# Ranks of the chosen keys: Sign on ScalarE with a table of biases, in place of comparisons of 2048 elements on VectorE

## The chip, the cores and the metric

The kernel runs on one core of one Trainium2 chip. The metric is the device time of one execution in microseconds (us), and a version is judged by the median of its runs. Engines are named as the profile names them: PE (TensorE), PEld (its weight loads), DVE (VectorE), ACT (ScalarE), POOL (GpSimd), SP (SyncE, which here only issues transfers).

## The reference, cut to what matters

Two layers, each of which adds a mixer of three kinds of attention and then an expert retrieval to `x` (256 tokens of 2048 numbers). The change sits in the retrieval. For each token and each of 8 heads it scores 128 keys twice, keeps the 16 best of each side, forms sums of pairs, keeps the 16 best pairs and turns each into the number of one of 16,384 experts:

```python
top_s, top_i = lax.top_k(s, PEER_TOPK)
cand_s = (top_s[..., 0, :, None] + top_s[..., 1, None, :]).reshape(..., 256)
cand_i = (top_i[..., 0, :, None] * PEER_KEYS + top_i[..., 1, None, :]).reshape(..., 256)
best_s, best_j = lax.top_k(cand_s, PEER_TOPK)
idx = jnp.take_along_axis(cand_i, best_j, axis=-1)
g = jax.nn.softmax(best_s, axis=-1)
...
a = jnp.einsum('td,tkd->tk', xt, u[it])
hsel = jax.nn.gelu(a) * gt
y = jnp.einsum('tk,tkd->td', hsel, vv[it])
```

## The kernel before, in words

**The stream of u.** The kernel does not gather the rows of `u`. In each layer it multiplies all 16,384 experts' rows with all 256 tokens: 128 blocks (`q`) of 128 experts, 1 MB each, loaded by SP into the tile `raw` (three buffers at most), and each block is worked in two half-blocks (`k`), 256 in a layer. A half-block is transposed on DVE (line 1274, `uT`), copied to a rounded high part on ACT (line 251, `hi`), has its low part formed by a subtraction on DVE or POOL (line 256, `lo`), and goes through 24 matmuls (lines 1308 and 1310, tile `acc`). After every second block ACT applies the gelu (line 1319, `at`) and the result is written to a large array `Gd` in device memory. Loads, preparation and matmuls run in the order of one loop, `run`: in each turn it prepares the half-block two ahead, multiplies the present one, and then calls `tick`.

**The routing beside it.** The choice of experts is a generator, `route`, put into the list `side`. `tick` runs it to its next `yield`, so a piece of routing stands between the half-blocks on every engine:

```python
def tick():
    for g in side[:SIDE_W[0]]:
        try:
            next(g)
        except StopIteration:
            side.remove(g)
```

So one `yield` is one half-block of the stream. While `r["routing"]` is set, the low parts of three half-blocks in four are formed on POOL, otherwise on DVE. `route` works the tokens in two halves (`hf`). Near the end of each half stand the lines that are changed: the position `bj` of each of the 16 chosen pairs of a head is taken apart into a rank on each side (`abf[:, 0]` the start of the row of pairs, `abf[:, 1]` the place in it), each rank is compared with 16 candidates (line 1019, 8 heads x 16 choices x 16 candidates = 2048 elements per partition, tile `oh`), the result is multiplied by the key numbers `tif` (line 1023) and summed (line 1033). For side 0 the comparison is "at least the start of the row", and `tif` holds differences of neighbouring keys, so that the sum is the wanted key; for side 1 it is equality. Lines 1036 and 1037 put both keys and the token together to `idx`, the address of one element of `Gd`.

**The scatter.** When both halves are done, three yields later, POOL issues one indirect DMA for each of 8 heads x 16 choices x 2 halves (line 1050, `Gd<-g,idx`), each of which adds 128 weights `g` into `Gd`: 256 in a layer, of which 32 are held back until six rows of `v` have been fetched (line 1360). Near the end of the stream, at block 122, SP loads the weights of the last three blocks back from `Gd` (line 1301, `gs`), and this load must wait for the scatter:

```python
if q == NQ - 6 and k == 0:
    gt = va["g"] = r["up"].tile([P, NS, T], F32, name="gs")
    for h in range(2):
        SP.dma_start(gt[:, :, h * P:(h + 1) * P], gav[0][:, NQ - NS:, h])
```

The loads of the later blocks of `u` stand behind it in SP's queue. Two more generators, `marks` (line 1123, `over`) and `lists` (lines 1207 to 1265), follow `route` and find out which experts were chosen; at block 108 `drain()` runs whatever is left of them at once. Then the stage of `v` begins.

Of the kernel before, what the change touches and what calls it, by code (L numbers as in the profile page):

```python
# [27 lines left out]
AF = mybir.ActivationFunctionType  # L28
OP = mybir.AluOpType
# [4 lines left out]
P = 128  # L34
# [7 lines left out]
E = 16384  # L42
NQ = E // P

C_ID, C_IO, C_TP, C_ST = 0, 128, 144, 146
NPERS = 162
NS = 3
NW = (NQ - NS) // 2 * 2
PRE = ((1, 0), (1, 1), (2, 0), (2, 1), (0, 0), (0, 1))
# [7 lines left out]
def shape_constants():  # L57
    pers = np.zeros((P, NPERS), np.float32)
    pers[:, C_ID:C_ID + P] = np.eye(P)
    pers[:, C_IO:C_IO + 16] = np.arange(16)  # L60
    pers[:, C_TP] = np.arange(P)
    pers[:, C_TP + 1] = np.arange(P) + T
    pers[:, C_ST:C_ST + 16] = [16 * a if a < 4 else 64 + 4 * (a - 4) for a in range(16)]
    mix = np.zeros((P, NMIX), np.float32)
    p = np.arange(P)
    inv = (10000.0 ** (-np.arange(32, dtype=np.float64) / 32)).astype(np.float32)
    ang = inv[p % 32][:, None] * np.arange(T, dtype=np.float32)[None, :]
    mix[:, M_COS:M_COS + T] = np.cos(ang.astype(np.float64))
    mix[:, M_SIN:M_SIN + T] = np.where((p % 64) < 32, -1.0, 1.0)[:, None] * np.sin(ang.astype(np.float64))
    for hf in range(2):  # L70
        dist = np.abs(p[:, None] + hf * P - np.arange(T)[None, :]).astype(np.float32)
        mix[:, M_DIST + hf * T:M_DIST + (hf + 1) * T] = np.where(dist <= 128, dist, 1e32)
    c = p % 64
    st = np.clip(c - 8, 0, 48)
    kc = np.arange(64)[None, :]
    ok = (kc >= st[:, None]) & (kc < st[:, None] + 16)
    mix[:, M_BM:M_BM + 64] = np.where(ok, 0.0, -1e30)
    m = np.arange(P)[None, :]
    k = p[:, None]
    mix[:, M_SW:M_SW + P] = (m // 64 == k // 64) & (m % 64 == (k % 64 + 32) % 64)  # L80
    mix[:, M_DUP:M_DUP + P] = (k < 64) & (m % 64 == k)
    mix[:, M_DSW:M_DSW + P] = (k < 64) & (m % 64 == (k + 32) % 64)
    mix[:, M_REV:M_REV + P] = (m // 64 == k // 64) & (m % 64 == 63 - k % 64)
    lst = np.zeros((P, NLST), np.float32)
    lst[:, L_LE:L_LE + P] = k <= m
    lst[:, L_GT:L_GT + P] = k > m
    lst[:, L_LT:L_LT + P] = k < m
    lst[:, L_IO:L_IO + 512] = np.arange(512)
    lst[:, L_JC:L_JC + P] = -(m * P + k + 0.5)
    lst[:, L_BA:L_BA + 32] = 512.0 * np.arange(32)  # L90
    return pers, mix, lst
# [3 lines left out]
def hybrid_parallel_heads_peer_encoder_kernel(ctx, tc, x, ln1, w_in, a_sink, b_rel_bias, c_q_norm, c_kv_norm,  # L95
# [4 lines left out]
    V, S, G, TE, SP = nc.vector, nc.scalar, nc.gpsimd, nc.tensor, nc.sync  # L100
# [16 lines left out]
    pers = pools.new("pers")  # L117
# [3 lines left out]

    CP = pers.tile([P, NPERS], F32, name="CP")
    SP.dma_start(CP, c_pers)
    ident = CP[:, C_ID:C_ID + P]
    iota16 = CP[:, C_IO:C_IO + 16]
    start16 = CP[:, C_ST:C_ST + 16]
    gains = pers.tile([P, 112], F32, name="gains")
    onecol = pers.tile([P, 1], F32, name="onecol")
    V.memset(onecol, 1.0)
# [740 lines left out]
    def peer(l, m):  # L870
        r = {}
# [46 lines left out]
        def evac_q(a):  # L918
            rp = r["rp"]
            qh = rp.tile([P, 8, T], F32R, name="qh", tag="oh0")  # L920
            ql = rp.tile([P, 8, T], F32R, name="ql", tag="oh1")
            r["routing"] = True
            side.append(route(a, qh, ql))
# [25 lines left out]
        def route(a, qh, ql):  # L949
# [19 lines left out]
            for hf in range(2):  # L969
                top = rp.tile([P, 8, 2, 16], F32, name="top", tag="top", bufs=2)  # L970
                ti = rp.tile([P, 8, 2, 16], U32, name="ti", tag="ti", bufs=2)
                tif = rp.tile([P, 8, 2, 16], F32, name="tif", tag="tif", bufs=2)
# [34 lines left out]
                abf = rp.tile([P, 2, 8, 16], F32, name="abf", tag="abf")  # L1007
# [2 lines left out]
                V.tensor_scalar(ab[:, 0], ab[:, 0], 3, None, op0=OP.bitwise_or)  # L1010
                V.tensor_tensor(ab[:, 1], bj, ab[:, 0], op=OP.bitwise_and)
                V.tensor_copy(abf[:, 1], ab[:, 1])
                V.tensor_tensor(tif[:, :, 0, 1:], ti[:, :, 0, 1:], ti[:, :, 0, :15], op=OP.subtract)
                i12 = rp.tile([P, 2, 8, 16], F32, name="i12", tag="i12")
                yield
                ohs = []
                for c in range(2):
                    oh = rp.tile([P, 8, 16, 16], F32, name="oh", tag=f"oh{c}")
                    V.tensor_tensor(oh, abf[:, c, :, :, None].to_broadcast([P, 8, 16, 16]),
                                    (iota16 if c else start16)[:, None, None, :].to_broadcast([P, 8, 16, 16]),  # L1020
                                    op=OP.is_equal if c else OP.is_ge)
                    yield
                    V.tensor_tensor(oh, oh, tif[:, :, c, None, :].to_broadcast([P, 8, 16, 16]), op=OP.mult)
                    ohs.append(oh)
                    yield
# [8 lines left out]
                    yield  # L1034
                i1, i2 = (i12[:, c].rearrange("p h k -> p (h k)") for c in range(2))
                V.scalar_tensor_tensor(i1, i1, 128.0, i2, op0=OP.mult, op1=OP.add)
                V.tensor_scalar(r["idx"][:, hf], i1, 512.0, CP[:, C_TP + hf:C_TP + hf + 1], op0=OP.mult, op1=OP.add)
                yield
                found.append((top, cand, best))
            r["routing"] = False  # L1040
# [516 lines left out]
```

## Time and profile before

| | us |
|---|---|
| runs of the kernel before (3) | 3339.32, 3327.32, 3314.28 |
| median | 3327.32 |
| the profiled execution: its own time | 3324.39 |
| the profiled execution: span from the first to the last instruction | 3322.6 |

The profile and all rows below are of the one profiled execution. It lies 2.93 us under the median of the runs, and the runs lie 25 us apart. Start times in the rows are us from the span's start; a window A:B means that stretch of the span. A row of a timeline gives the start, the time the instructions took, engine, line, operation, what it writes and reads, and in brackets how long the engine had been idle before it and for what. Idle time of an engine that nothing waits for costs nothing.

### The profile page before, as it was taken

The numbers are of one execution on the slowest core, as the hardware profiler recorded it, in microseconds if no ns is written. First come the engines' busy times: TensorE is split into PE (matmuls) and PEld (weight loads), VectorE is DVE, ScalarE is ACT, GpSimd is POOL, SyncE is SP. The second block draws the span as 40 slices with busy tenths as digits, with TensorE's granted clock in tenths as the row PEclk, the third lists the DMA queues.
The fourth block names the chain that finished last, engine by engine and source line by source line (L and its number), as shares of the span: only waits on it lengthen the run. The fifth ranks groups of instructions, "written<-read, shape, count | busy, mean of one in ns | idle before, by whom it ended". The sixth has DMA issues, their size and how long they took to land. (4 is left out here: it accounts for less than half of the span.)

```text
span 3322.6 us, 58212 instructions
## 1 busy us (share of the span) xinstructions
PE 3085.5 (93%) x21677; PEld 2852.7 (86%) x21677; DVE 2439.9 (73%) x3613; ACT 1701.7 (51%) x2827; POOL 1805.3 (54%) x1135
## 2 busy tenths in 40 slices
PE   8998998999999977999999989999899999889998
PEld 8997898899999976888889977989899998877886
DVE  6676578987879855777776666599977787667776
ACT  5554443356757424555554544433576564345554
POOL 3110045588888873666531010365788888736662
PEclk9999999999999988999999999999999999999999
DMA  5677688899999996888835776988899999968885
GB/s 193 197 219 212 169 182 180 184 180 190 185 186 201 177 210 219 338 312 302 301 124 179 231 182 191 195 184 179 178 182 189 183 199 172 228 198 331 303 310 180
DMA packets 438648, 702.14 MB, mean 211 GB/s; under 512 B 104568, under 2 KB 237384, under 8 KB 414088
## 3 DMA queue, kind: packets, MB, share of 16 engines
q1 hardware_dynamic: 256912, 434.08, 54.3%
q0 software_dynamic: 112304, 228.13, 23.8%
q10 hardware_dynamic: 69064, 35.36, 4.4%
q8 instruction: 190, 3.11, 0.4%
q14 instruction: 178, 1.46, 0.2%
HBM read 627.95 MB, written 69.47 MB: 210 GB/s over the span
## 5 line engine op out<-in xcount | busy, mean ns | idle before, releaser
L1308 PE MATMUL acc<-x2h,hi 128*128 128x256 f32 x4096 | 1012.2, 286 | 31.0 <-ACT hi L251 15.3
L1050 POOL DMA_INDIRECT Gd<-g,idx x512 | 928.8, 1814 | 171.1 <-issue 151.7
L1308 PE MATMUL acc<-x2l,hi 128*128 128x256 f32 x4096 | 997.2, 282 | 0.3 <-issue 0.3
L251 ACT ACTIVATE hi<-uT 128x1024 fp32r<-128x1024 f32 x512 | 543.2, 1061 | 725.9 <-DVE uT L1274 616.0
L1274 DVE STREAM_TRANSPOSE uT<-raw 128x1024 f32<-128x1024 f32 x512 | 634.9, 1240 | 303.1 <-DMA raw<-in_peer_u_dram 217.3
L1308 PEld LDWEIGHTS acc<-x2h,hi 128*128 128x128 f32 x4096 | 783.5, 191 | 37.2 <-ACT hi L251 20.0
L1308 PEld LDWEIGHTS acc<-x2l,hi 128*128 128x128 f32 x4096 | 781.9, 191 | 1.3 <-issue 1.3
L1310 PE MATMUL acc<-x2h,lo 128*128 128x256 f32 x4096 | 583.5, 285 | 99.2 <-DVE lo L256 76.3
L1310 PEld LDWEIGHTS acc<-x2h,lo 128*128 128x128 f32 x4096 | 523.2, 191 | 119.1 <-DVE lo L256 87.1
L166 DVE TENSOR_TENSOR vl<-vr,vh 128x1024 fp32r<-128x1024 f32 x356 | 425.8, 1223 | 140.9 <-ACT vh L165 133.9
L256 POOL TENSOR_TENSOR lo<-uT,hi 128x1024 fp32r<-128x1024 f32 x116 | 302.5, 2609 | 395.2 <-DMA raw<-in_peer_u_dram 194.0
L256 DVE TENSOR_TENSOR lo<-uT,hi 128x1024 fp32r<-128x1024 f32 x396 | 470.0, 1187 | 21.4 <-PE acc L1310 11.3
L165 ACT ACTIVATE vh<-vr 128x1024 fp32r<-128x1024 f32 x356 | 366.5, 1054 | 141.0 <-PE y L156 129.7
L152 PE MATMUL y<-vh,dh 128*128 128x512 f32 x1032 | 406.6, 394 | 18.8 <-ACT vh L165 13.5
L256 DVE TENSOR_TENSOR lo<-raw,hi 128x1024 fp32r<-128x1024 f32 (+1 forms) x240 | 291.5, 1222 | 160.8 <-ACT hi L251 60.2
L156 PE MATMUL y<-vh,dl 128*128 128x512 f32 x1032 | 405.2, 393 | 0.0
L251 ACT ACTIVATE hi<-raw 128x1024 fp32r<-128x1024 f32 (+1 forms) x240 | 245.4, 1034 | 239.7 <-DMA raw<-in_w_o_dram 79.3
L1360 POOL DMA_INDIRECT vr<-in_peer_v_dram,iv x160 | 217.1, 1357 | 172.5 <-ACT vh L165 78.9
L161 PE MATMUL y<-vl,dh 128*128 128x512 f32 x1032 | 294.4, 392 | 0.3
L152 PEld LDWEIGHTS y<-vh,dh 128*128 128x128 f32 x1032 | 196.0, 190 | 63.4 <-ACT vh L165 22.7
L161 PEld LDWEIGHTS y<-vl,dh 128*128 128x128 f32 x1032 | 194.8, 189 | 43.0 <-DVE vl L166 2.5
L156 PEld LDWEIGHTS y<-vh,dl 128*128 128x128 f32 x1032 | 196.1, 190 | 40.9
(400 smaller groups left out, 4268.4 us busy)
## 6 DMA issues: line engine op xcount, KB each, us to landing
raw<-in_peer_u_dram SPq DMA_DIRECT2D x1024, 256.0 KB
raw<-in_w_in_dram SPq DMA_DIRECT2D x64, 512.0 KB
Gd<-z SPq DMA_DIRECT2D x32, 1024.0 KB
raw<-in_w_o_dram SPq DMA_DIRECT2D x32, 1024.0 KB
Gd<-at ACTq DMA_DIRECT2D x124, 256.0 KB
raw<-in_w_in_dram SPq DMA_DIRECT2D x64, 256.0 KB
raw<-in_peer_w_q_dram SPq DMA_DIRECT2D x64, 256.0 KB
raw<-in_w_in_dram SPq DMA_DIRECT2D x32, 416.0 KB
```

What stands on the lines that cost most here:

```text
L152: TE.matmul(o, lh, rh, start=start, stop=False, skip_group_check=shared)
L156: TE.matmul(o, ll, rh, start=False, stop=False, skip_group_check=shared)
L161: TE.matmul(o, lh, rl, start=False, stop=stop, skip_group_check=shared)
L165: S.activation(hi, src, AF.Copy)
L166: V.tensor_tensor(lo, src, R32(hi), op=OP.subtract)
L251: S.activation(view(h), src, AF.Copy)
L256: (eng or V).tensor_tensor(view(lo), src, R32(view(h)), op=OP.subtract)
L1050: d = G.indirect_dma_start(out=Gd[:], out_offset=bass.IndirectOffsetOnAxis(ap=r["idx"][:, hf, i:i + 1], axis=0), in_=r["g"][:, hf, i:i + 1 ...
L1274: V.transpose(t.rearrange("p (c e i) -> p c e i", c=8, e=4), rv.rearrange("p e (c j) -> p c e j", c=8))
L1308: TE.matmul(o, hi[:, c * P:(c + 1) * P], xx, start=k == 0 and c == 0 and n == 0, stop=False)
L1310: TE.matmul(o, lo[:, c * P:(c + 1) * P], xT(k * 8 + c)[0], start=False, stop=k == 1 and c == 7)
L1360: G.indirect_dma_start(out=raw, out_offset=None, in_=peer_v.rearrange("l e d -> (l e) d"), in_offset=at_(r[iv][:, c, m:m + 1]))
```

## The change: what it does

The two comparisons of 2048 elements on DVE go. In their place ACT fills `oh` in 16 slices for each side, one for each candidate `k`: `Sign(abf + bias_k)`, with the bias 0.5 minus the candidate read from a new table in the constants (`C_SB`, 32 columns of the tile `CP`). Each such instruction has 128 elements per partition and writes them 16 elements apart. A sign is +1 or -1, so both sides now use differences of neighbouring keys, with the first entry of `tif` the sum of the first and the last key; the sum is then twice the wanted key, and line 1037's factor 512 becomes 256. A `yield` stands after every eighth Sign, so that a side has three yields where it had two.

```diff
-                V.tensor_tensor(tif[:, :, 0, 1:], ti[:, :, 0, 1:], ti[:, :, 0, :15], op=OP.subtract)
+                V.tensor_tensor(tif[:, :, :, 1:], ti[:, :, :, 1:], ti[:, :, :, :15], op=OP.subtract)
+                V.tensor_tensor(tif[:, :, :, 0], ti[:, :, :, 0], ti[:, :, :, 15], op=OP.add)
                 i12 = rp.tile([P, 2, 8, 16], F32, name="i12", tag="i12")
                 yield
                 ohs = []
                 for c in range(2):
                     oh = rp.tile([P, 8, 16, 16], F32, name="oh", tag=f"oh{c}")
-                    V.tensor_tensor(oh, abf[:, c, :, :, None].to_broadcast([P, 8, 16, 16]),
-                                    (iota16 if c else start16)[:, None, None, :].to_broadcast([P, 8, 16, 16]),
-                                    op=OP.is_equal if c else OP.is_ge)
-                    yield
+                    for k in range(16):
+                        S.activation(oh[:, :, :, k], abf[:, c], AF.Sign,
+                                     bias=CP[:, C_SB + 16 * c + k:C_SB + 16 * c + k + 1])
+                        if k % 8 == 7:
+                            yield
                     V.tensor_tensor(oh, oh, tif[:, :, c, None, :].to_broadcast([P, 8, 16, 16]), op=OP.mult)
                     ohs.append(oh)
                     yield
...
-                V.tensor_scalar(r["idx"][:, hf], i1, 512.0, CP[:, C_TP + hf:C_TP + hf + 1], op0=OP.mult, op1=OP.add)
+                V.tensor_scalar(r["idx"][:, hf], i1, 256.0, CP[:, C_TP + hf:C_TP + hf + 1], op0=OP.mult, op1=OP.add)
```

The table of biases, and its place in the constants:

```diff
-C_ID, C_IO, C_TP, C_ST = 0, 128, 144, 146
-NPERS = 162
+C_ID, C_IO, C_TP, C_ST, C_SB = 0, 128, 144, 146, 162
+NPERS = 194
...
+    pers[:, C_SB:C_SB + 16] = 0.5 - pers[:, C_ST:C_ST + 16]
+    pers[:, C_SB + 16:C_SB + 32] = 0.5 - np.arange(16)
```

How the instructions stand on ACT in the first layer, first half of the tokens, from the Exp of the routing on; before:

```order
L1005 ACT_TABLE_LOAD
L1005 ACTIVATE e<-e 128x128
L251 ACTIVATE hi<-uT 128x1024 x3
L1319 ACT_TABLE_LOAD
L1319 ACTIVATE at<-acc 128x512
L1325 DMA Gd<-at 512x1x128
L251 ACTIVATE hi<-uT 128x1024 x4
```

and now, where line 1321 is what was line 1319:

```order
L1005 ACT_TABLE_LOAD
L1005 ACTIVATE e<-e 128x128
L251 ACTIVATE hi<-uT 128x1024
L1021 ACTIVATE oh<-abf,CP 128x128 x8
L251 ACTIVATE hi<-uT 128x1024
L1021 ACTIVATE oh<-abf,CP 128x128 x8
L251 ACTIVATE hi<-uT 128x1024
L1321 ACT_TABLE_LOAD
L1321 ACTIVATE at<-acc 128x512
L1327 DMA Gd<-at 512x1x128
L251 ACTIVATE hi<-uT 128x1024
L1021 ACTIVATE oh<-abf,CP 128x128 x8
```

Each batch of eight Signs stands between two high parts of the stream; a fourth batch follows one `hi` later. The number of table loads in the whole program is the same in both, and none stands at a Sign.

On DVE at the same place, from the last step of the ranks to the weights' sum `rden`; before:

```order
L1013 TENSOR_TENSOR tif<-ti 128x8x15
L1274 STREAM_TRANSPOSE uT<-raw 128x1024
L1019 TENSOR_TENSOR oh<-abf,CP 128x2048
L1274 STREAM_TRANSPOSE uT<-raw 128x1024
L256 TENSOR_TENSOR lo<-uT,hi 128x1024
L1023 TENSOR_TENSOR oh<-oh,tif 128x2048
L1274 STREAM_TRANSPOSE uT<-raw 128x1024
L1019 TENSOR_TENSOR oh<-abf,CP 128x2048
L1274 STREAM_TRANSPOSE uT<-raw 128x1024
L1023 TENSOR_TENSOR oh<-oh,tif 128x2048
L1274 STREAM_TRANSPOSE uT<-raw 128x1024
L1027 TENSOR_REDUCE rden<-e 128x8
```

and now (1276 is what was 1274, 1025 what was 1023, 1029 what was 1027):

```order
L1013 TENSOR_TENSOR tif<-ti 128x16x15
L1014 TENSOR_TENSOR tif<-ti 128x16
L1276 STREAM_TRANSPOSE uT<-raw 128x1024 x2
L256 TENSOR_TENSOR lo<-uT,hi 128x1024
L1276 STREAM_TRANSPOSE uT<-raw 128x1024
L1025 TENSOR_TENSOR oh<-oh,tif 128x2048
L1276 STREAM_TRANSPOSE uT<-raw 128x1024 x3
L256 TENSOR_TENSOR lo<-uT,hi 128x1024
L1025 TENSOR_TENSOR oh<-oh,tif 128x2048
L1276 STREAM_TRANSPOSE uT<-raw 128x1024
L1029 TENSOR_REDUCE rden<-e 128x8
```

Five transposes of the stream stood between `tif` and `rden`; now there are seven.

On POOL in the first layer, from the clearing of the lists to the first scatter; before:

```order
L256 TENSOR_TENSOR lo<-uT,hi 128x1024 x10
L968 MEMSET ie 128x768
L968 MEMSET iv 128x768
L256 TENSOR_TENSOR lo<-uT,hi 128x1024 x48
L1049 ISA
L1050 DMA Gd<-g,idx 8389120x1
```

and now:

```order
L256 TENSOR_TENSOR lo<-uT,hi 128x1024 x10
L968 MEMSET ie 128x768
L968 MEMSET iv 128x768
L256 TENSOR_TENSOR lo<-uT,hi 128x1024 x51
L1051 ISA
L1052 DMA Gd<-g,idx 8389120x1
```

The first scatter stands four half-blocks of the stream later, and three of their low parts are POOL's.

## Rows read from the trace of the kernel before

**Rows 1.** The page's first part: busy us (share of the span) x instructions
```profile
PE 3085.5 (93%) x21677; PEld 2852.7 (86%) x21677; DVE 2439.9 (73%) x3613; ACT 1701.7 (51%) x2827; POOL 1805.3 (54%) x1135
```
**Rows 2.** Windows: length, busy us (instructions) of PE, PEld, DVE, ACT, POOL, clock, DMA, GB/s
```profile
547.00:576.00 29.00, 21.72 (x170) 20.28 (x170) 28.90 (x23) 10.31 (x11) 17.88 (x6) 1.00 0.85 177
...
685.00:1160.00 475.00, 453.83 (x3943) 445.74 (x3943) 392.74 (x485) 294.62 (x669) 407.59 (x222) 0.99 0.99 187
```
**Rows 3.** SP's queue, waits in window 1200:1260: us in total, times, longest
```profile
SPq L1301 <- DMA Gd<-g,idx: 12.7, 1, 12.7
```
**Rows 4.** The same in window 2880:2930, the second layer
```profile
SPq L1301 <- DMA Gd<-g,idx: 0.2, 1, 0.2
```
**Rows 5.** Timeline of SP's queue at the load of gs, first and second layer
```profile
1249.00 0.93 SPq L1301 DMA_DIRECT2D gs<-Gd  x2
...
2919.08 0.92 SPq L1301 DMA_DIRECT2D gs<-Gd  x2
```
**Rows 6.** Timeline of POOL: first and last scatter of each layer
```profile
684.91 1.73 POOL L1050 DMA_INDIRECT Gd<-g,idx  x1 [0.20 <-issue]
...
1245.53 2.08 POOL L1050 DMA_INDIRECT Gd<-g,idx  x1 [0.30 <-issue]
...
2361.22 1.71 POOL L1050 DMA_INDIRECT Gd<-g,idx  x1 [0.19 <-issue]
...
2913.37 1.56 POOL L1050 DMA_INDIRECT Gd<-g,idx  x1 [0.30 <-issue]
```
**Rows 7.** Groups of POOL in 680:1260: busy, mean ns, idle before and why
```profile
L1050 POOL DMA_INDIRECT Gd<-g,idx x256 | 468.7, 1831 | 86.7 <-issue 75.8 <-DMA vr<-in_peer_v_dram,ivr 9.9 <-DMA Gd<-g,idx 0.3
```
**Rows 8.** Timeline of DVE behind the wait for the scatter, first layer
```profile
1258.22 1.25 DVE L1274 STREAM_TRANSPOSE uT<-raw 128x1024 f32<-128x1024 f32 x1 [12.04 <-DMA raw<-in_peer_u_dram]
```
**Rows 9.** Timeline of DVE at the changed lines, first layer, first half
```profile
547.49 1.23 DVE L1274 STREAM_TRANSPOSE uT<-raw 128x1024 f32<-128x1024 f32 x1
548.65 2.24 DVE L1019 TENSOR_TENSOR oh<-abf,CP 128x2048 f32<-128x2048 f32 x1
...
553.08 2.28 DVE L1023 TENSOR_TENSOR oh<-oh,tif 128x2048 f32<-128x2048 f32 x1
...
556.44 3.30 DVE L1019 TENSOR_TENSOR oh<-abf,CP 128x2048 f32<-128x2048 f32 x1
...
560.83 3.29 DVE L1023 TENSOR_TENSOR oh<-oh,tif 128x2048 f32<-128x2048 f32 x1
564.04 1.23 DVE L1274 STREAM_TRANSPOSE uT<-raw 128x1024 f32<-128x1024 f32 x1
```
**Rows 10.** Timeline of ACT at the same place
```profile
548.82 1.06 ACT L251 ACTIVATE hi<-uT 128x1024 fp32r<-128x1024 f32 x1 [2.37 <-DVE uT L1274]
...
557.71 1.28 ACT L1319 ACT_TABLE_LOAD   x1
559.00 0.60 ACT L1319 ACTIVATE at<-acc 128x512 f32<-128x512 f32 x1
```
**Rows 11.** Timeline of ACT later, a high part and four Relus with a bias
```profile
766.84 1.06 ACT L251 ACTIVATE hi<-uT 128x1024 fp32r<-128x1024 f32 x1 [2.62 <-DVE uT L1274]
767.80 1.27 ACT L1123 ACTIVATE over<-s_sb,nb 128x128 bf16<-128x128 f32 x4
```
**Rows 12.** Groups of ACT, shapes kept apart: busy us, mean ns of one
```profile
L251 ACT ACTIVATE hi<-uT 128x1024 fp32r<-128x1024 f32 x512 | 543.2, 1061 | 725.9 <-DVE uT L1274 616.0 <-issue 43.5 <-PE acc L1310 32.5
...
L1123 ACT ACTIVATE over<-s_sb,nb 128x128 bf16<-128x128 f32 x512 | 162.4, 388 | 19.7 <-ACT at L1319 17.3 <-issue 2.4
...
L1005 ACT ACTIVATE e<-e 128x128 f32<-128x128 f32 x4 | 1.2, 312 | 0.0
```
**Rows 13.** Groups of DVE, shapes apart; the first reads elements 16 bytes apart
```profile
L1092 DVE TENSOR_TENSOR below<-cand,best 128x384 f32<-128x384 f32 x4 | 3.4, 842 | 0.0
...
L1092 DVE TENSOR_TENSOR below<-cand,best 128x512 f32<-128x512 f32 x4 | 2.7, 680 | 0.0
```
**Rows 14.** Transfers issued in window 685:1160: KB each
```profile
raw<-in_peer_u_dram SPq DMA_DIRECT2D x300, 256.0 KB
```

More of the change, by code (lines that the diff above doesn't have):

```diff
@@ L124, in hybrid_parallel_heads_peer_encoder_kernel @@
     ident = CP[:, C_ID:C_ID + P]
-    iota16 = CP[:, C_IO:C_IO + 16]
-    start16 = CP[:, C_ST:C_ST + 16]
     gains = pers.tile([P, 112], F32, name="gains")
```

## The prediction

> **What bounds the kernel now.** The page's first part comes first: PE is busy for 93% of the span [rows 1], which reads like a kernel bound by matmuls. The windows say something else for the stage that the change touches. Around the changed lines DVE is busy for 28.90 of 29.00 us while PE has 21.72; later in the same stage, where the scatter runs, the 16 DMA engines are busy to 0.99 and DVE to 393 of 475 us [rows 2]. So DVE sets the pace for some 30 us in each half of the tokens, and transfers set it behind that.
>
> What ends the stage is a third thing, and the waits of SP's queue show it. In the first layer the load of `gs` waits 12.7 us for the scatter [rows 3] and goes out at 1249.00 [rows 5]; the loads of `u` behind it come late, and DVE then stands idle for 12.04 us [rows 8]. In the second layer the same load waits 0.2 us [rows 4]. The timeline of POOL shows why: the scatter starts at 684.91 and its last instruction at 1245.53, one behind the other [rows 6], 256 of 1.831 us with 86.7 us between them [rows 7]. That is a chain of 563 us (1245.53 + 2.08 - 684.91) which nothing shortens when the rest is faster, and it hangs on the end of the routing. What the change does to the time is therefore read from one number: when the first scatter can start.
>
> How much each layer feels of it: in the first layer the load of `gs` goes out 1.39 us behind the end of the last scatter (1249.00 - 1247.61), and SP was waiting, so a later scatter is a later end, one for one. In the second the last scatter ends at 2914.93; with the same 1.39 us it would have let the load go at 2916.3, and the load went at 2919.08 [rows 5, 6]. So the second layer has 2.8 us to spare.
>
> **The change part by part.** *Removed from DVE:* two comparisons in each half and layer, eight in all, 2.24 us where POOL is quiet and 3.30 us where its subtraction runs beside them [rows 9]. The four turns of the stream with a comparison or a multiplication in them took 564.04 - 547.49 = 16.55 us [rows 9].
>
> *Added to DVE:* the sum for the first entry of `tif`, and 240 elements for 120 in the difference. By the smallest rows of this kind I put both at 0.35 us a half, in front of everything that follows, so it counts.
>
> *Added to ACT:* 32 Signs a half. The nearest row is the Relu of line 1123: the same 128 elements, the same bias from a column. One takes 388 ns [rows 12], four in a row 1.27 us [rows 11], so each further one takes (1.27 - 0.388) / 3 = 0.294 us, and eight behind a `hi` lengthen the queue by 8 x 0.294 = 2.35 us. A `hi` takes its place for 0.96 us (767.80 - 766.84) [rows 11].
>
> *The new chain.* ACT has only 10.31 of 29.00 us of work there [rows 2], which looks like cover. But the Signs come in four batches between five `hi`, and in ACT's order the table load and the gelu stand among them. From the first `hi` at 548.82 [rows 10]: `hi` and eight Signs twice, 2 x (0.96 + 2.35) = 6.6, to 555.4; then the multiplication on DVE, 2.28 [rows 9], and the next transpose, 1.23, to 558.9 (ACT does a `hi`, the table load of 1.28 and the gelu of 0.60 [rows 10] in that time); again twice `hi` and eight Signs, 6.6, to 565.5; the second multiplication, 2.3 to 3.3, to 567.8 or 568.8. It ended at 564.04. With the 0.35 us that is 4.1 to 5.1 us later in each half; I take 4.8. Meanwhile six half-blocks went by and not four, so nothing of the stream is lost: what is lost is that the routing's next pieces stand two half-blocks later.
>
> *Bounds of this term.* Below: if the Signs vanish behind the stream, six turns go by at its pace. In the window of the scatter 300 quarter-megabyte loads, 150 half-blocks, took 475 us [rows 14], 3.17 us each; six are 19.0 us, 2.5 more than 16.55, with the 0.35 us 2.8. Above: the Signs write one element in each 64 bytes, which no row of ACT shows. On DVE, line 1092 takes 680 ns for 512 neighbouring elements, and the comparison of 2048 took 2.24 us, so 1.02 ns an element; 384 would take 550 ns, but where they are read 16 bytes apart they take 842 [rows 9, 13], 0.76 ns an element more. If ACT's writes pay the same, a Sign takes 0.10 us more, 32 take 3.1, and a half is 7.9 us later. I keep 4.8, since the Relu's row has the same engine, operand and size. [...]
>
> *The scatter itself.* Its instructions last longer when DVE runs beside them: their mean is 1.831 us [rows 7] against 1.56 us for the quick ones [rows 6], 69 us in all over the 563 / 3.17 = 178 half-blocks that run beside it. Four fewer are beside it now, which gives back 4 x 0.39 = 1.6 us.
>
> *At nothing:* the 16 KB of constants more at the start, since the transfer is short and the start is not what the stage ends on; the Signs' tables, as the built program has as many table loads as before; and the four half-blocks by which `marks` and `lists` end later. Their last step stood four turns ahead of `drain` and now falls into it, the first piece there; nothing queues up, and POOL still has scatters to do then. If that cover were gone, the six fetches of `v` would wait for the lists.
>
> **The sum.** In each layer the scatter starts 2 x 4.8 = 9.6 us later and runs 1.6 us shorter: 8.0. The first layer pays 8.0, the second 8.0 - 2.8 = 5.2, together 13. Against the profiled execution's own 3324.39 that is 3337.6; that execution lies 2.9 us under the median of the runs, so I predict **3340 us**, 0.4% slower.
>
> **The rivals.** *The stream sets the end, and DVE's relief counts (not slower).* The changed lines are where DVE is full, and DMA stands at 0.85 there against 0.99 later [rows 2]. If transfers could make up that difference over the two stretches of some 29 us in each layer, (0.99 - 0.85) x 29 x 4 = 16 us would come off: 3308 against the profiled execution, 3311 against the median. It decides if the load of `gs` no longer waits, that is if the scatter, started later, still ends before SP gets there. Against it: in the first layer it would have to end 12.7 us earlier, and it hangs on the same routing. I give it 0.12.
>
> *Writes 64 bytes apart are dear.* At the upper bound above, 7.9 us a half: (15.8 - 1.6) + (15.8 - 1.6 - 2.8) = 25.6, 3350, or 3353 against the median. If each element cost four times the 0.84 ns that `hi` shows ((1061 - 312) ns over 896 elements [rows 12]), a Sign would take 0.32 us more, a half 10.3 us: 15.1 us a half, 54 in all, 3382. [...] I give the first 0.22 and the second 0.05. The first is a matter of size, the sign stays.
>
> *The Signs hide.* At 2.8 us a half, the scatter starts 5.6 us later, 4.0 net; the first layer pays 4.0, the second 1.2: 3330, or 3333 against the median. What speaks for it is ACT's idle time [rows 2]; against it that a multiplication waits for 16 Signs in a row. Chance 0.15.
>
> **How the numbers follow.** My own case has 0.46, and these are all. Runs of the kernel before lie within 25 us, so a measurement can hardly tell less than 1% (33 us) from no change. Against the median, the likeliest cases span 3333 to 3353; a median of three such runs may move by some 10 us to either side, which gives **3323 to 3363**. Within that range lie my case, the hiding and most of the first dear case; outside are the gain and the dearest writes, under 2 in 10. Slower by over 1% (above 3360.6) holds the dearest writes, a part of the first dear case and of the noise: 0.11. Faster by over 1% needs twice what the first rival gives: 0.03. Within 1%: 0.86.
>
> **What would show it.** Right: the first multiplication on DVE waits for Signs; the Signs' mean is 0.39 us; `rden` follows the last step of `tif` some 5 us later than it did; the first scatter starts some 10 us later after the stream's first transpose; SP's wait at `gs` is near 22 us in the first layer and 7 in the second. Wrong: no wait at `gs` (the first rival), Signs of 0.5 us or more (the second), or a scatter whose own length changes by more than a few us, since I hold it fixed. The prediction would also fail if the time behind `gs` were not passed on one for one.

## The result, and the profile after

The changed kernel takes 3352.21 us (3343.72 to 3366.13), the kernel before, beside it on the same chip, 3331.37 us (3314.28 to 3348.75). The ratio is 1.0064, with a 95% interval of 1.0043 to 1.0085: slower by 21 us, between 14 and 28. That is inside the range of the prediction and on its side, but more than its 13 us. The profiled execution has a span of 3347.6 us, 25.0 more than before.

The first part of the page, busy us of each engine, answers to [rows 1]. DVE gave up 26.7 us (2439.9 - 2413.2) and ACT took 37.6 more (1739.3 - 1701.7), which is 128 x 0.294:

```profile
PE 3099.3 (93%) x21677; PEld 2869.1 (86%) x21677; DVE 2413.2 (72%) x3603; ACT 1739.3 (52%) x2955; POOL 1808.7 (54%) x1141
```

Windows of the changed kernel, columns as in [rows 2]:

```profile
547.00:576.00 29.00, 23.16 (x182) 21.93 (x183) 22.21 (x21) 21.82 (x46) 16.97 (x7) 1.00 0.87 188
685.00:1160.00 475.00, 447.54 (x3840) 437.83 (x3839) 384.73 (x481) 289.75 (x665) 402.44 (x224) 0.99 0.96 183
```

Around the changed lines DVE is busy for 22.21 of 29.00 us where it was full with 28.90, and the transfers rise from 0.85 to 0.87 (177 to 188 GB/s). So the engine that set the pace there was relieved, and in this window the stream went a little faster. Little of that lasts: by the 89th of its 256 transposes in a layer it is later than before (below).

What ends the stage is read as before. Waits of SP's queue at the load of `gs`, now line 1303, in windows 1200:1300 and 2900:2960 (us in total, times, longest), answering to [rows 3, 4]:

```profile
SPq L1303 <- DMA Gd<-g,idx: 10.2, 1, 10.2
...
SPq L1303 <- DMA Gd<-g,idx: 9.6, 1, 9.6
```

Timeline of SP's queue at that load in both layers [rows 5]:

```profile
1252.88 0.93 SPq L1303 DMA_DIRECT2D gs<-Gd  x2
...
2943.69 0.92 SPq L1303 DMA_DIRECT2D gs<-Gd  x2
```

Timeline of POOL, first and last scatter of each layer [rows 6]:

```profile
700.61 1.73 POOL L1052 DMA_INDIRECT Gd<-g,idx  x1 [0.20 <-issue]
...
1249.58 1.91 POOL L1052 DMA_INDIRECT Gd<-g,idx  x1 [0.30 <-DMA Gd<-g,idx]
...
2385.39 1.71 POOL L1052 DMA_INDIRECT Gd<-g,idx  x1 [0.19 <-issue]
...
2940.65 1.68 POOL L1052 DMA_INDIRECT Gd<-g,idx  x1 [0.30 <-issue]
```

The starts are to be counted from the first transpose of the stream of `u` in their layer. That stands at 419.83 and 2099.20 before and at 423.17 and 2109.52 after. So the scatter starts 277.4 and 275.9 us behind it, where it was 265.1 and 262.0: 12.4 and 13.9 us later. Now both layers wait at `gs`, and the second one did not. The last transpose of `u` follows 17.2 and 17.7 us behind that load (1270.05 and 2961.36); before, in the layer that waited, it was 16.4 (1265.41). So where SP waits, the end of the scatter sets the end of the stage.

Timeline of DVE at the changed lines, first layer, first half [rows 9] and then second half:

```profile
550.25 2.36 DVE L1276 STREAM_TRANSPOSE uT<-raw 128x1024 f32<-128x1024 f32 x2
...
558.44 2.29 DVE L1025 TENSOR_TENSOR oh<-oh,tif 128x2048 f32<-128x2048 f32 x1 [3.27 <-ACT oh L1021]
...
568.78 2.29 DVE L1025 TENSOR_TENSOR oh<-oh,tif 128x2048 f32<-128x2048 f32 x1 [0.93 <-ACT oh L1021]
570.99 1.24 DVE L1276 STREAM_TRANSPOSE uT<-raw 128x1024 f32<-128x1024 f32 x1
...
660.84 1.24 DVE L1276 STREAM_TRANSPOSE uT<-raw 128x1024 f32<-128x1024 f32 x1
...
671.65 2.29 DVE L1025 TENSOR_TENSOR oh<-oh,tif 128x2048 f32<-128x2048 f32 x1 [4.65 <-ACT oh L1021]
...
683.24 2.29 DVE L1025 TENSOR_TENSOR oh<-oh,tif 128x2048 f32<-128x2048 f32 x1 [3.23 <-ACT oh L1021]
685.45 1.24 DVE L1276 STREAM_TRANSPOSE uT<-raw 128x1024 f32<-128x1024 f32 x1
```

Each multiplication waits for Signs, which is a wait that the kernel before did not have. The first half takes 570.99 - 550.25 = 20.7 us where it took 16.55; the second 685.45 - 660.84 = 24.6 where the trace of before has 16.56. Timeline of ACT in that second half shows why it is dearer [rows 10]:

```profile
663.27 1.28 ACT L1321 ACT_TABLE_LOAD   x1
664.56 0.60 ACT L1321 ACTIVATE at<-acc 128x512 f32<-128x512 f32 x1
665.19 0.52 ACTq L1327 DMA_DIRECT2D Gd<-at  x1
665.76 2.56 ACT L1021 ACTIVATE oh<-abf,CP 128x128 f32<-128x128 f32 x8 [0.60 <-ACT at L1321]
668.13 1.04 ACT L251 ACTIVATE hi<-uT 128x1024 fp32r<-128x1024 f32 x1
669.07 2.54 ACT L1021 ACTIVATE oh<-abf,CP 128x128 f32<-128x128 f32 x8
...
679.47 0.57 ACT L1321 ACTIVATE at<-acc 128x512 f32<-128x512 f32 x1
680.07 0.52 ACTq L1327 DMA_DIRECT2D Gd<-at  x1
680.64 2.57 ACT L1021 ACTIVATE oh<-abf,CP 128x128 f32<-128x128 f32 x8 [0.60 <-ACT at L1321]
```

In the first half the table load and the gelu stand between two multiplications, while DVE has stream to do. Here the table load, the gelu and its transfer stand right ahead of the first batch, and a second gelu with its transfer ahead of the last one. In both places DVE is the one that waits.

Groups of ACT, shapes apart (busy us, mean ns), answering to [rows 12]:

```profile
L1125 ACT ACTIVATE over<-s_sb,nb 128x128 bf16<-128x128 f32 x512 | 162.3, 388 | 19.5 <-ACT at L1321 19.5
...
L1021 ACT ACTIVATE oh<-abf,CP 128x128 f32<-128x128 f32 x128 | 40.9, 494 | 2.4 <-ACT at L1321 2.4
```

A Sign lasts 494 ns, 106 more than the Relu. But eight behind one another take 2.54 to 2.57 us, so each further one costs (2.56 - 0.494) / 7 = 0.295 us, the Relu's own step. Signs overlap, and what a single one lasts longer is paid once in eight.

### The profile page after: what moved, and what is told of

Its sections match the earlier page's. It is cut to its first block, busy times and chain, and to the rows that moved or that the text cites. A ratio compares the mean times of both kernels' runs of the same rounds, so it can differ in the third digit from the quotient of the medians.

```text
span 3347.6 us, 58338 instructions
## 1 busy us (share of the span) xinstructions
PE 3099.3 (93%) x21677; PEld 2869.1 (86%) x21677; DVE 2413.2 (72%) x3603; ACT 1739.3 (52%) x2955; POOL 1808.7 (54%) x1141
```

## The experiments

Three parts of the change can be told apart: each half has two turns more (a comparison had one `yield`, 16 Signs have two), ACT's queue has 32 Signs more, and DVE waits for them. Ratios are to the kernel before, timed on the same chip.

**The turns alone.** The kernel before, with one turn more behind each comparison:

```diff
                                     op=OP.is_equal if c else OP.is_ge)
                     yield
+                    yield
                     V.tensor_tensor(oh, oh, tif[...], op=OP.mult)
```

> The kernel before with one more yield behind each comparison, so that the routing takes four half-blocks more in each layer and nothing else changes: the comparisons stay on DVE. Theory (the scatter is a chain that begins later by the half-blocks that were added): a turn of the stream without routing work takes some 3 us, so the first scatter starts 4 x 3 = 12 us later after the stream's first transpose in each layer, and the time rises by 12 to 21 us (some 0.4 to 0.6%), as with the whole change. Rival (the Signs on ACT are what costs): within 5 us of the kernel before.

Ratio 1.0037 [1.0021, 1.0054], 12 us, at the lower end of what was expected. Timeline of DVE, first half of layer 1, the transposes ahead of and behind the changed lines:

```profile
551.85 1.23 DVE L1275 STREAM_TRANSPOSE uT<-raw 128x1024 f32<-128x1024 f32 x1
...
573.34 1.24 DVE L1275 STREAM_TRANSPOSE uT<-raw 128x1024 f32<-128x1024 f32 x1
```

That is 21.5 us, 4.9 more than before; the second half takes 22.0 (686.42 - 664.45), 5.4 more. The scatter starts 277.1 and 273.5 us behind the stream's first transpose, as late as in the changed kernel, while the stream itself is on time: the 89th transpose stands 289.4 and 285.8 us behind the first, before 289.1 and 286.1. Waits of SP's queue in both layers:

```profile
SPq L1302 <- DMA Gd<-g,idx: 6.3, 1, 6.3
...
SPq L1302 <- DMA Gd<-g,idx: 5.6, 1, 5.6
```

So with no Sign in the program the turns alone cost over half of the loss. The two starts are 12.0 and 11.5 us late; less the 1.6 us a layer and the 2.8 us of slack of the prediction that would cost 17.5 us one for one, and it costs 12 (7 to 18, so 17.5 is just within it). The lists, too, end four turns later here; that is taken up below.

**Signs in the turns of before.** All 16 Signs of a comparison in one turn:

```diff
-                        if k % 8 == 7:
+                        if k == 15:
                             yield
```

> The changed kernel with all 16 Signs of a side ahead of one yield, so that the routing takes as many half-blocks as before and only the move to ACT is left. Theory (start of the scatter): ACT's queue is 4.7 us longer per side and DVE waits for it, 2 to 4 us a half, so the scatter starts 4 to 8 us later in each layer and the time rises by 4 to 12 us: about half of the change. Rival (the Signs hold the high parts of the stream back, and the stream sets the end): as slow as the change, 20 us, since ACT has the same work in fewer turns. Second rival (DVE's relief counts): faster than before.

Ratio 1.0107 [1.0088, 1.0126]: 36 us slower, where the theory had 4 to 12 and the dearer rival 20. The scatter starts at 276.1 and 273.7 with no turn added, because the stream as a whole falls back: at the 89th transpose it is 11 us late (300.2 us behind the first, in layer 1). Timeline of ACT and, apart, of DVE in the first half:

```profile
554.16 4.88 ACT L1021 ACTIVATE oh<-abf,CP 128x128 f32<-128x128 f32 x16
...
566.20 4.89 ACT L1021 ACTIVATE oh<-abf,CP 128x128 f32<-128x128 f32 x16 [0.60 <-ACT at L1321]
```

```profile
559.08 2.29 DVE L1025 TENSOR_TENSOR oh<-oh,tif 128x2048 f32<-128x2048 f32 x1 [3.56 <-ACT oh L1021]
...
571.13 2.29 DVE L1025 TENSOR_TENSOR oh<-oh,tif 128x2048 f32<-128x2048 f32 x1 [6.25 <-ACT oh L1021]
```

The theory that only the turns count falls here. While DVE stands for 3.56 and 6.25 us, no transpose is made, and behind 4.88 us of Signs no `hi`.

**The load of `gs` off SP's queue.** In the kernel before, and in the changed one:

```diff
-                        SP.dma_start(gt[:, :, h * P:(h + 1) * P], gav[0][:, NQ - NS:, h])
+                        G.dma_start(gt[:, :, h * P:(h + 1) * P], gav[0][:, NQ - NS:, h])
```

> The kernel before, with the load of gs issued by POOL behind its scatters instead of by SP, so that the loads of the last blocks of u no longer queue behind the wait for the scatter. Theory: SP's wait (12.7 and 0.2 us in the profile) goes, and 5 to 13 us come off (0.15 to 0.4%). Rival (the wait is only where the slack shows, the stage ends on transfers anyway): no change.

> The changed kernel with the same load of gs on POOL. Theory: the later scatter costs time only through SP's wait, so 15 to 20 us come off the change and it stands within 5 us of the kernel before with the same edit. Rival (the Signs or the longer routing slow the stream itself): it stays some 20 us slower than the kernel before with the same edit.

The first: 0.9946 [0.9931, 0.9961], 3318.3 us, faster than both kernels and 18 us (13 to 23) under the kernel before, where 5 to 13 were expected. That is more than the 12.9 us that SP waits at `gs` in the profile of before; where the rest comes from isn't shown. The second: 1.0007 [0.9993, 1.002], still 0.6% slower than the first, so by the rival, where within 5 us was expected. Timeline of POOL at that load in layer 1, of the first and then of the second:

```profile
1252.43 1.67 POOL L1301 DMA_DIRECT2D gs<-Gd  x2 [8.58 <-DMA Gd<-g,idx]
```

```profile
1270.34 1.67 POOL L1303 DMA_DIRECT2D gs<-Gd  x2 [5.97 <-DMA Gd<-g,idx]
```

The last transpose of `u` stands at 1262.14 in the first, so `gs` goes out ahead of it; in the second at 1263.0, and `gs` goes out 7 us later than that. The late scatter then ends on the stage of `v`: from the last transpose of layer 1 to the first of layer 2 it takes 842.4 us instead of 833.0, and DVE waits 8.0 us for `gs` there. The pair shows what moving the load is worth; it doesn't take the scatter off the path, as it was meant to.

**Half of the scatter.** This does take it off, in both kernels:

```diff
-            for h, hf in todo[:-HELD]:
+            for h, hf in todo[:6]:
```

> The kernel before with half of the scatter left out (8 of its 16 groups of a layer, so half of the weights are missing in the output). The chain of scatters then ends long before the load of gs. Theory: the wait at gs is gone and transfers are fewer, so the time is 10 us or more under the kernel before. It is the base for the next kernel.

> The changed kernel with the same half of the scatter left out. Theory (the change costs because the scatter starts later): with the scatter off the path it stands within 8 us of the base, where the change had 20. Rival (the Signs slow the stream of u itself, by the high parts that queue behind them on ACT): it stays 15 us or more slower than the base.

0.9947 [0.9929, 0.9964] and 0.9987 [0.9969, 1.0005]. Without a wait at `gs` in either, the changed kernel is still 0.40% slower, some 13 us, between the 8 of the theory and the 15 of the rival. Timeline of DVE, last transpose of `u` in layers 1 and 2, first kernel and then second:

```profile
1263.39 1.25 DVE L1274 STREAM_TRANSPOSE uT<-raw 128x1024 f32<-128x1024 f32 x1
...
2934.13 1.25 DVE L1274 STREAM_TRANSPOSE uT<-raw 128x1024 f32<-128x1024 f32 x1
```

```profile
1270.98 1.25 DVE L1276 STREAM_TRANSPOSE uT<-raw 128x1024 f32<-128x1024 f32 x1
...
2948.21 1.25 DVE L1276 STREAM_TRANSPOSE uT<-raw 128x1024 f32<-128x1024 f32 x1
```

Counted from the first transposes (422.18 and 2098.41; 423.26 and 2105.83) the stages take 841.2 and 835.7 against 847.7 and 842.4, so 6.5 and 6.7 us more. My theory that the change is paid by the scatter alone falls with this.

**Signs without the turns.** The Signs in four batches of eight, one a turn; the first multiplication in the turn of the fourth batch, the second one turn later, so that a half has as many turns as before:

```diff
+                    for k in range(16):
+                        S.activation(ohs[c][:, :, :, k], ...)
+                        if k % 8 == 7:
+                            if c == 1 and k == 15:
+                                weigh(0)
+                            yield
...
+                weigh(1)
```

> The changed kernel with its pieces grouped anew: four batches of eight Signs in four yields, the first multiplication with the fourth batch, the second with the weights' sum, so that a half takes as many yields as before and no multiplication follows directly behind its Signs. Theory: the scatter starts within 4 us of where it started before (265.1 us after the first transpose), and the time is within 8 us of the kernel before. Rival (any Signs on ACT cost, however they are grouped): 15 us or more slower.

> The regrouped kernel with the load of gs on POOL. Theory: within 5 us of the kernel before with that edit, which stood 0.54% under the kernel before; if DVE's relief is worth anything where the scatter no longer holds the stream, it is a few us faster still. Rival (the Signs slow the stream): 10 us or more slower than it.

1.0038 [1.0023, 1.0053], and with `gs` on POOL 0.9974 [0.996, 0.9989], which is 0.28% (9 us) above the kernel before with the same edit, with intervals that just touch. The scatter starts 267.4 and 264.8 us behind the first transpose, 2.3 and 2.8 later than before, so the turns explained nearly all of its lateness. Yet 12 us are lost, more than the 8 of the theory. The stream's 89th transpose stands 2.3 and 2.8 us late. With the first experiment this makes a table of two by two: nothing 1, turns alone 1.0037, Signs alone 1.0038, both 1.0064. ("Signs alone" also has its multiplications in other turns.)

**Late lists.** With half of the scatter, four empty turns ahead of the lists in the kernel before; and in the changed kernel four turns fewer in `bounds`, so that the lists end where they did:

```diff
+            for _ in range(4):
+                yield
             yield from lists(cnt)
```

```diff
                     V.tensor_tensor(o, cv, best[...], op=OP.is_lt)
-                yield
                 V.tensor_scalar(m, m, -NEG, None, op0=OP.mult)
```

> Half of the scatters is left out, as in the kernel before with half a scatter, so the output lacks those weights. Four empty turns of the stream stand ahead of the lists, so that their last step stands in the piece of half-block 216 as in the changed kernel; there are no Signs, and the routing ends where it did. Theory L (the late lists at the opening of the fetches of v cost what is left without the scatter): a ratio to the kernel before of 0.9985 to 1.001, like the changed kernel with half a scatter (0.9987), so 3330 to 3338 us, and 7 us more a layer from the first transpose of the stream to the last than the 841 and 836 us of the kernel before with half a scatter. Rival S (the Signs' waits in the stream cost it): 0.9947 within 0.0015, near 3320 us.

> Half of the scatters is left out, as before. The changed kernel, with two pieces of the bounds put in one turn (four turns fewer in all), so that the last step of the lists stands four half-blocks ahead of the opening again, as in the kernel before; the Signs stay. Theory L: 0.994 to 0.996, some 3320 us, and 841 and 836 us between first and last transpose. Rival S: 0.9987 within 0.0015, near 3335 us.

0.9974 [0.9963, 0.9986] and 1.0001 [0.9989, 1.0013]. The first lies above its own base (0.9947) by 0.27%, 9 us, with intervals that just touch, and so between the two theories; the second doesn't come down towards that base, as theory L asked, but stays with its own (0.9987). In the profiles the stage of the first takes 840.1 and 836.4 us, like its base; that of the second 846.6 and 839.7, near its own. But the profiled execution of the first is one of its quickest (3318.36 us, median 3326.08), so it doesn't speak against the 9 us. By the second kernel late lists are not what is left without the scatter. Whether they cost some us of their own, and so have a part in the price of the turns, stays open.

**Neighbouring writes.** Each Sign writes 128 neighbouring elements, and DVE reads them with steps:

```diff
-                    oh = rp.tile([P, 8, 16, 16], ...)
+                    oh = rp.tile([P, 16, 8, 16], ...)
-                        S.activation(oh[:, :, :, k], abf[:, c], AF.Sign,
+                        S.activation(oh[:, k], abf[:, c], AF.Sign,
```

> The changed kernel, with each Sign writing 128 neighbouring elements, and the multiplication and the sum reading with steps. If the 0.49 us of a Sign alone comes from the writes 64 bytes apart: 0.39 us, like the Relu. If it comes from the function: 0.49 still. Eight in a row take 2.35 to 2.45 us in the first case. What the rest pays shows on DVE: the multiplication, 2.29 us now, up to 3.9 us by the 0.76 ns an element of steps, and the sums likewise. Time of the whole: within 0.004 of the changed kernel's ratio of 1.0064, as what the chain of a half wins on ACT (0.1 us a batch) it loses on DVE.

Groups of ACT, and of DVE, shapes apart (busy us, mean ns):

```profile
L1021 ACT ACTIVATE oh<-abf,CP 128x128 f32<-128x128 f32 x128 | 39.0, 388 | 2.4 <-ACT at L1321 2.4
```

```profile
L1025 DVE TENSOR_TENSOR oh<-oh,tif 128x2048 f32<-128x2048 f32 x8 | 18.3, 2293 | 23.1 <-ACT oh L1021 23.1
...
L1035 DVE TENSOR_REDUCE i<-oh 128x128 f32<-128x2048 f32 x8 | 30.5, 3807 | 0.0
```

The Sign lasts 388 ns like the Relu: the 106 ns are the price of the 64-byte step, not of the function. Eight still take 2.43 us. The multiplication takes 2293 ns, as in the changed kernel, the sum 3807 ns where that has 2245. Ratio 1.014 [1.0118, 1.0162], where 1.0064 within 0.004 was expected. The sums make the routing 4 x 1.56 = 6.2 us longer in each layer, and the scatter starts 6.7 and 5.5 us later than in the changed kernel (284.2 and 281.4 us); SP waits 25.0 and 14.7 us at `gs`. The later starts account for about half of the 25 us more than in the changed kernel. In the profiles the rest is the scatter's own length, 565.8 and 561.3 us against 550.9 and 556.9: start and length together give 21.6 and 9.9 us, and the stages are 21.8 and 9.4 longer. Why it is longer isn't shown.

**Signs that nothing waits for.** The kernel before, with its comparisons, and 32 Signs a half besides in the places where the regrouped kernel has them; the result goes to a buffer that nothing reads:

```diff
+                    sg = rp.tile([P, 8, 16], F32, name="sg", tag="sg")
+                    for k in range(8):
+                        S.activation(sg, abf[:, c], AF.Sign, bias=CP[:, C_IO + k:C_IO + k + 1])
                     V.tensor_tensor(oh, abf[...], op=OP.is_equal if c else OP.is_ge)
                     yield
+                    for k in range(8, 16):
+                        S.activation(sg, abf[:, c], AF.Sign, bias=CP[:, C_IO + k:C_IO + k + 1])
                     V.tensor_tensor(oh, oh, tif[...], op=OP.mult)
```

> The kernel before, with its comparisons on VectorE, and in addition the 32 Signs a half on ScalarE in the places where the regrouped kernel has them; their results go to a small buffer that nothing reads, and no turn is added. ScalarE's order is the regrouped kernel's, VectorE's that of the kernel before. Theory Q (the Signs hold the stream's own work in ScalarE's queue): a ratio to the kernel before of 1.003 to 1.006, so at least what the regrouped kernel showed (1.0038), and the stream 2 to 5 us late by half-block 100. Theory W (it is VectorE's wait for the Signs that costs): 0.999 to 1.0015, the stream on time, within 1 us of the kernel before at half-block 88.

Ratio 1.0035 [1.0017, 1.0054], by theory Q. Timeline of ACT in the first half, then of POOL and DVE behind it, then the same of the kernel before, and last DVE at the first and the 89th transpose of layer 1:

```profile
564.35 3.45 ACT L1020 ACTIVATE sg<-abf,CP 128x128 f32<-128x128 f32 x8 [0.60 <-ACT at L1324]
567.70 1.04 ACT L251 ACTIVATE hi<-uT 128x1024 fp32r<-128x1024 f32 x1
568.64 3.43 ACT L1027 ACTIVATE sg<-abf,CP 128x128 f32<-128x128 f32 x8
571.98 1.99 ACT L251 ACTIVATE hi<-uT 128x1024 fp32r<-128x1024 f32 x2
```

```profile
568.82 2.37 POOL L256 TENSOR_TENSOR lo<-uT,hi 128x1024 fp32r<-128x1024 f32 x1 [3.46 <-ACT hi L251]
...
569.10 2.23 DVE L1034 TENSOR_TENSOR g<-e,rden 128x128 f32<-128x128 f32 x1
...
573.06 1.23 DVE L256 TENSOR_TENSOR lo<-uT,hi 128x1024 fp32r<-128x1024 f32 x1 [0.58 <-ACT hi L251]
```

```profile
562.07 4.29 POOL L256 TENSOR_TENSOR lo<-uT,hi 128x1024 fp32r<-128x1024 f32 x1
...
565.72 0.79 DVE L1029 TENSOR_TENSOR g<-e,rden 128x128 f32<-128x128 f32 x1
```

```profile
424.04 1.25 DVE L1279 STREAM_TRANSPOSE uT<-raw 128x1024 f32<-128x1024 f32 x1 [4.04 <-DMA raw<-in_peer_u_dram]
...
716.92 1.25 DVE L1279 STREAM_TRANSPOSE uT<-raw 128x1024 f32<-128x1024 f32 x1
```

The transpose for the `hi` at 567.70 ended at 564.27, but that `hi` stands behind eight Signs, which stand behind the gelu. So POOL's subtraction starts late and lies on DVE's small multiplication `g`. In both kernels `g` ends 0.14 or 0.15 us behind POOL's subtraction; here that makes it 1.44 us longer, and DVE waits 0.58 us more for the next `hi`. Together these are 2.0 of the 2.1 us that the transposes fall behind there (from 567.42 to 576.40, before from 564.04 to 570.88).

The 89th stands 292.9 us behind the first, 3.8 late, and 5.4 in layer 2 (2392.16 - 2100.71 against 286.1); the scatter starts 3.7 and 5.4 later, with no turn added and nothing on DVE that waits for a Sign. Signs that only stand in ACT's queue hold up `hi`, and with it the stream and the routing that shares its turns. The dose was larger than meant: eight into one buffer take 3.44 us, not 2.56. So it shows the mechanism, and that Signs which nothing waits for can cost 12 us; of the changed kernel's own share the regrouped kernel is the better measure. The profiled execution is the quickest of its runs (3337.38 us, median 3349.74), so the trace doesn't show where all of the 12 us go.

## Why the prediction was right, and where its terms were off

**What ends the stage: right, and both layers now show it.** The load of `gs` waits for the scatter in both, and by the first experiment a later start is passed on, one for one at most. The waits forecast, 22 and 7 us, came out as 10.2 and 9.6 for two reasons. In the first layer the scatter itself was 11.8 us shorter, so it ended only 0.5 us later behind the first transpose. And SP came to the load 3.0 and 4.9 us later in its layer: a stream that is late eats up its wait. The wait alone was a poor measure; with the idle Signs there is none in the first layer and 0.4 us in the second, and that kernel is slower too.

**A half costs 4.8 us: right for the first (4.2 and 0.2 for `tif`), wrong for the second (8.1 and 0.2).** In the first half the chain came out as worked: from the first `hi` to the transpose behind the second multiplication it was to take 19.0 to 20.0 us and took 19.4 (570.99 - 551.58). The failing step is the working from one half, doubled. I followed ACT's order only in the half of [rows 10]; the place of the table load and of the gelus differs in the other. Summed, 12.7 us a layer instead of 9.6, and the scatter starts 12.4 and 13.9 later. The first experiment adds that the Signs' queue is not needed for that: two more turns, with the comparisons left on DVE, make a half 4.9 and 5.4 us longer and the start as late. With the turns taken out and the Signs kept, the start is only 2.3 and 2.8 us late.

**"Nothing of the stream is lost": this is the step that failed.** I counted ACT's idle time as cover, and the half-blocks that go by as full pace. But a `hi` behind eight Signs comes up to 2.56 us late, and what follows it on POOL and DVE shifts, as the last experiment shows. At the 89th transpose the stream is 0.6 and 2.1 us late in the changed kernel, 2.3 and 2.8 in the regrouped one, 3.8 and 5.4 with the idle Signs, and with the turns alone it is on time. The waits in the window of [rows 2] don't show it: POOL waits 14.7 us for `hi` there and 13.6 before, PE 6.9 us for `hi` and `lo` together and 7.1 before. What is new in that window is that DVE waits, 4.2 us for Signs and 2.4 us for POOL.

The regrouped kernel puts a price of 12 us on Signs without turns; half a scatter puts 13 us on what is left without it. The late stream, 2 to 3 us a layer at the 89th transpose, is under half of that. In the regrouped kernel's own trace most of the rest stands in the second layer, where the scatter itself takes 565.6 us against 553.7 before. It is 561.1 to 565.6 in the four layers of the regrouped kernel and of that with `gs` on POOL, and 553.7 to 562.7 in the four of the kernel before and of that with `gs` on POOL. Whether the Signs or chance make it longer, four layers against four can't tell, and what the 13 us are without the scatter stays open too: in the kernel before, the two layers alone differ by 7 us behind the 101st transpose (521.3 and 514.4). TensorE's granted clock is a rival for the late stream: in window 655:690 it is 0.90 in the changed kernel and 1.00 before. Against it, the kernel before with `gs` on POOL has 0.95 there and in 548:582, and its 89th transposes are on time (288.9 and 285.9 us behind the first).

**The scatter's own length, held fixed: it isn't.** It was 562.7 and 553.7 us, and is 550.9 and 556.9, though the prediction named such a change as a sign of being wrong; its group in window 680:1260 answers to [rows 7]:

```profile
L1052 POOL DMA_INDIRECT Gd<-g,idx x256 | 462.3, 1806 | 79.6 <-issue 75.8 <-DMA vr<-in_peer_v_dram,ivr 2.2 <-DMA Gd<-g,idx 0.6
```

The 1.6 us that I gave it for fewer transposes beside it are far below this variation. It hid the loss in the first layer's stage of this one execution (846.9 us, before 845.6), while the second grew from 838.5 to 851.8.

**The price of a Sign.** One lasts 0.49 us, as the bound that I estimated from DVE's reads had it (0.10 us more); in a queue it is 0.295, as the Relu had it (0.294). The runs show the 106 ns more, 494 against 388, where the writes are 64 bytes apart and not where they are neighbours; how they come about isn't shown. In a row the difference is nearly hidden: eight take 2.56 against 2.43 us.

**The sum and the rivals.** 13 us forecast, 21 measured; the side and the range hold, the sum lacks a term for the held stream. The gain from DVE's relief is excluded: the interval begins at 1.0043, and with half a scatter, where nothing waits for its end, the relief is there and the time is longer too. Signs that hide fall with the regrouped kernel. The dear writes would have given 3353, close to 3352.21, and are wrong all the same: eight Signs cost what I had put for them, so that the nearness is luck. The missing 8 us are put down to the second half and to the held stream; how much is whose isn't shown. With the measured starts in place of mine the sum would even come out, (12.4 - 1.6) + (13.9 - 1.6 - 2.8) = 20.3; but that is no proof of it. The same sum gives 17.5 for the turns alone, which cost 12 (7 to 18), and next to nothing for the regrouped Signs, (2.3 - 1.6) and less than the slack, which cost 12 (8 to 18). The table of two by two holds better: 12 and 12 make 24, where both together show 21, within the interval.

## What to carry to other kernels

An engine that is busy for 10.31 of 29.00 us is no cover if work of the stream stands in its queue: what matters is what stands right behind the added instructions, and who waits for that. A cooperative schedule charges twice for a longer step, in turns for its own chain and in place for everybody else's; count both, and for each repetition, since the neighbours in the queue differ. And try the wait first that the profile names: one load moved to another queue gave 0.5% here, and the change that relieved the engine that was full around the changed lines cost 0.6%.

## What the runs showed of the hardware

- An ACTIVATE of 128 elements that writes 64 bytes apart lasts 494 ns against 388 for neighbours, but in a row both step by 0.29 to 0.295 us.
- The same ACTIVATE, eight times into one and the same buffer, steps by (3.44 - 0.40) / 7 = 0.43 us: there the step is longer than the 0.40 us of a single one, so these did not overlap, while writes to different places did.
- DVE's multiplication of 2048 elements takes 2.29 us in both layouts of the Signs; its sum over 16 takes 2245 ns over neighbours and 3807 over elements 512 bytes apart.
- DVE's multiplication `g` of 128 elements takes from 0.79 us, in the kernel before, to 2.34, in the regrouped one: beside POOL's subtraction it ends 0.14 or 0.15 us behind it, in the changed kernel, the kernel before and the one with idle Signs (first half, first layer).
